# A down projection in passes of 256 tokens instead of 512

## The chip, the cores and the metric

The kernel runs on one NeuronCore of a Trainium2 chip. The metric is the time of one execution on the device, in microseconds (us). Three runs of the kernel before took 884.18, 884.53 and 885.38 us, so the median is 884.53 us. A fourth execution was recorded by the hardware profiler, and every line called a line of the profile comes from it.

Engine names are those of the profile: PE is the matrix engine and PEld its weight loads, DVE the vector engine, ACT the scalar engine, POOL the general one, and SP the engine that issues most DMAs. PSUM is the memory that PE writes its products to; it is cut into banks of 512 fp32 numbers per partition.

## The reference

One decoder layer in fp32, with 512 tokens and 1024 model columns. It has two feed-forward blocks (SwiGLU) with a mixing stage between them. Cut to what matters here:

```python
D_MODEL, SEQ = 1024, 512
D_FF = 256 * math.ceil(8 * D_MODEL / 3 / 256)            # 2816 = 22 tiles of 128

def swiglu(x, w_gate, w_up, w_down):
    return (jax.nn.silu(x @ w_gate) * (x @ w_up)) @ w_down

x = x + 0.5 * swiglu(rms_norm(x, g_ffn1), w_ffn1_gate, w_ffn1_up, w_ffn1_down)
h = rms_norm(x, g_mix); proj = h @ w_in
x = x + concat([attention(proj), conv(proj), memory_attention(proj, mem)]) @ w_out
x = x + 0.5 * swiglu(rms_norm(x, g_ffn2), w_ffn2_gate, w_ffn2_up, w_ffn2_down)
```

The change touches only `... @ w_down`, the down projection of both blocks.

## The kernel before, in words

**Layout.** Activations lie transposed, features in partitions and tokens along the row: `x` is 8 tiles of 128 features by 512 tokens. A product of a weight tile (128 by 128, loaded into PE) with an activation tile streams the tokens past the weights; one such instruction is called a pass here, and its width is the number of tokens.

**Three passes for fp32.** Each fp32 operand is split into a high part in the type `float32r` and the rest, `hi` and `lo` (`whi`/`wlo` for weights; `xh`/`xl`, `hh`/`hl`, `bh`/`bl` for activations). A product is then `whi*hi + whi*lo + wlo*hi`, three passes into the same PSUM bank. The function `mm3` (line 334) does this for a list of contraction tiles `k`; its passes are lines 337, 338 and 339. Before every pass PE loads that pass's weights, also where the pass before used the same ones.

**A feed-forward block** (`ffn`, line 389) walks over 22 hidden tiles `f`. The first 4 are plain: 8 contraction tiles by three passes of 512 tokens for gate and as many for up. The other 18 go through `fast` (line 443), which works on blocks of 256 tokens: seven products of 4 contraction tiles by 3 passes, all of width 256, made by `product` (line 434, passes on lines 439, 440 and 441). Their results go to PSUM banks that ACT copies out (lines 450, 454, 456, 468, tiles called `kept`) and DVE combines (lines 459, 470, 474). The hidden tile is split into `hh` and `hl` (lines 397, 398), 512 tokens each.

**The down projection** (`down`, line 479) is cut into six rounds of 4, 4, 4, 4, 2 and 4 hidden tiles. In each round every one of the 8 tiles `d` of `x` takes one bank from a ring of four (`mm_bank`), gets `mm3` over the round's hidden tiles, and DVE adds half of the bank to `x` (line 496). A step over 4 hidden tiles is thus 12 passes. The steps of a round are spread over the hidden tiles `f` of the next round, between the products of `fast`; the last round comes at the end of the block. In the very last step of the kernel (tile 7, last round, second block) the tokens are already cut in two: two banks, one for each half of the tokens, 12 passes of width 256 each.

**Weights** come by DMA in pieces of 128 by 1024 fp32, are split by ACT (line 165, `whi`) and DVE (line 166, `wlo`) a few pieces ahead of use, and lie in a ring of four pairs of buffers. The start of a buffer is shifted by 0 or 128 bytes (`off`); `fast` and `down` both use 128. In the built program the tiles `hh`, `hl`, `bh` and `bl` all start at byte 320 modulo 512 of their partition, also at token 256, and the weight tiles of both stages at byte 128 or 384 modulo 512.

**Order.** The code is written for a tile framework that puts each engine's instructions in order by its own estimate of when each can run, and sets the semaphores. PE, DVE and ACT each run their instructions strictly in that order.

Of the kernel before, what the change touches and what calls it, by code (L numbers as in the profile page):

```python
# [38 lines left out]
P = 128  # L39
T = 512  # L40
# [146 lines left out]
def per_load(r):  # L187

    return 8 // (ROUNDS[r][1] - ROUNDS[r][0])
# [14 lines left out]
def layer(tc, ctx, a):  # L204
    nc = tc.nc
    PE, ACT, DVE, POOL = nc.tensor, nc.scalar, nc.vector, nc.gpsimd
# [12 lines left out]
    def mm_bank():  # L219
        return psum.tile([P, T], F32, tag="mm", name=nm("mm"), bufs=4)  # L220
# [7 lines left out]
    def work():  # L228
        return tmp.tile([P, T], F32, tag="t", name=nm("t"), bufs=5)
# [101 lines left out]
            DVE.tensor_tensor(yy, yy, h, op=ALU.mult)  # L331
            DVE.scalar_tensor_tensor(out, yy, 1.5, out, op0=ALU.add, op1=ALU.mult)

    def mm3(ps, wh, wl, ks, hi, lo, first, last, woff=0):
        for i, k in enumerate(ks):
            w = slice((k - woff) * P, (k - woff + 1) * P)
            PE.matmul(ps, wh[:, w], hi(k), start=first and i == 0, stop=False)  # L337
            PE.matmul(ps, wh[:, w], lo(k), start=False, stop=False)  # L338
            PE.matmul(ps, wl[:, w], hi(k), start=False, stop=last and i == len(ks) - 1)  # L339

    xhk = lambda k: xh[k]
    xlk = lambda k: xl[k]
# [1 line left out]
    def scaled_split(d, gcol):  # L344

        g = par[:, gcol + d : gcol + d + 1]
        xh[d], xl[d] = atile("xh"), atile("xl")
        ACT.activation(xh[d], x[:, d], AF.Identity, scale=g)
        DVE.scalar_tensor_tensor(xl[d], x[:, d], g, xh[d].bitcast(F32), op0=ALU.mult, op1=ALU.subtract)  # L349
# [39 lines left out]
    def ffn(pool, norm, first, gain, hooks, next_gain, last):  # L389
# [89 lines left out]
        def down(r, g):  # L479

            lo, hi = ROUNDS[r]
            end = r == len(ROUNDS) - 1
            wh, wl = W.next()

            def step(j):
                d = g * per_load(r) + j
                cut = last and end and d == KT - 1
                for t0, t1 in [(0, T // 2), (T // 2, T)] if cut else [(0, T)]:
                    ps = mm_bank()[:, : t1 - t0]
                    mm3(  # L490
                        ps, wh, wl, range(lo, hi), lambda k: h_hi[k][:, t0:t1], lambda k: h_lo[k][:, t0:t1],
                        True, True, woff=lo - j * (hi - lo),
                    )
                    xd = x[:, d, t0:t1]
                    o = work()[:, : t1 - t0] if last and end else xd
                    DVE.scalar_tensor_tensor(o, ps, 0.5, xd, op0=ALU.mult, op1=ALU.add)  # L496
                    if last and end:
                        nc.sync.dma_start(a["out"][d, :, t0:t1], o)
                if end and not last:
                    nxt.add(d)  # L500
                    scaled_split(d, next_gain)

            return [lambda j=j: step(j) for j in range(per_load(r))]
# [4 lines left out]
        for f in range(NF):  # L508
# [4 lines left out]
            if f >= N_DIRECT:  # L513
                fast(f, mid)
            else:
                g, u = (sc_bank(), sc_bank()) if f % 3 == 2 else (mm_bank(), mm_bank())
                gh, gl = W.next()
                if f == 0:
                    uh, ul = W.next()
                    for ks in first:  # L520
                        mm3(g, gh, gl, ks, xhk, xlk, ks[0] == 0, ks[-1] == 7)
                        mm3(u, uh, ul, ks, xhk, xlk, ks[0] == 0, ks[-1] == 7)
                    norm.stats()
                    held = (g, u)
                else:
                    mm3(g, gh, gl, range(8), xhk, xlk, True, True)
                    if f == 1:
                        norm.spread()
                        raw[0] = evac(0, *held)
                        blocks(0)  # L530
                        hidden(0, raw[0])
                    uh, ul = W.next()
                    mm3(u, uh, ul, range(8), xhk, xlk, True, True)
                    raw[f] = evac(f, g, u)
                    if f == 1:
                        hidden(1, raw[1])
                    blocks(f)
                if f == N_DIRECT - 1:
                    for i in range(2, N_DIRECT):
                        hidden(i, raw[i])  # L540
# [666 lines left out]
```

## Time and profile before

| | us |
|---|---|
| median of three runs | 884.53 |
| the profiled execution | 884.99 |
| its span, first to last instruction | 883.2 |
| PE busy | 869.9 (98%) |
| PE weight loads busy | 760.4 (86%) |
| DVE busy | 713.1 (81%) |
| ACT busy | 438.2 (50%) |

Matmuls overlap in the profile: each is shown with its whole latency, so the busy times of groups on PE add up to more than the span. What a pass costs in a stream of passes is the distance from its start to the start of the next. Rows of the timeline give starts in us with two decimals; over a run of many passes, first start to last start divided by the number of passes is exact to a fraction of a nanosecond.

The two feed-forward blocks take most of the span: their passes over hidden tiles begin at 59.0 us in the first block and about 584 us in the second, and the mixing stage lies between about 370 and 517 us.

### The profile page before, as it was taken

Reading aid. Unit: us, or ns where it says so; the run is one execution under the profiler, and the core shown is the slowest. Engines: PE = TensorE matmul, PEld = TensorE weight load, DVE = VectorE, ACT = ScalarE, POOL = GpSimd, SP = SyncE. Lnnn points to the kernel's source line nnn. Section 1 sums busy time; section 2 is a strip of 40 time slices with the busy share of each in tenths; the row PEclk is TensorE's granted clock in tenths of the full one; section 3 lists DMA queues with packets and bytes.
Section 4 is the critical chain, followed back from the end, with each engine's and each line's share of the span. In section 5 each row is a group of like instructions: output and inputs, shape, how many; then the busy total and the mean of one; then the engine's idle time right before and its main releaser. Section 6 shows DMA issues by size and latency. Waiting matters only on the chain.

```text
span 883.2 us, 13993 instructions
## 1 busy us (share of the span) xinstructions
PE 869.9 (98%) x5522; PEld 760.4 (86%) x5525; DVE 713.1 (81%) x1121; ACT 438.2 (50%) x733; POOL 45.9 (5%) x38
## 2 busy tenths in 40 slices
PE   7999999999999999999999999999999999999998
PEld 3889999899999999888666788889999999989997
DVE  7999978986796886769999776999987878777872
ACT  6454554454563445533929754345554444534540
POOL 6000000000020000300020021000000000000000
PEclk9999999999999999999999999999999999999999
DMA  5522333333334244231010232323334332332312
GB/s 196 167 96 86 106 120 108 109 108 119 119 121 129 87 120 144 72 101 60 4 57 13 84 100 92 96 72 124 104 107 120 96 118 85 111 117 72 120 48 96
DMA packets 34082, 88.45 MB, mean 100 GB/s; under 512 B 3168, under 2 KB 7008, under 8 KB 34016
## 3 DMA queue, kind: packets, MB, share of 16 engines
q1 hardware_dynamic: 32864, 85.99, 30.9%
q10 hardware_dynamic: 1152, 1.57, 0.6%
q8 instruction: 43, 0.70, 0.3%
q14 instruction: 23, 0.19, 0.1%
HBM read 85.45 MB, written 2.10 MB: 99 GB/s over the span
## 4 chain that ended last, share of the span: by engine, by line
PE 93%; DVE 4%; DMA 1%; issue 1%; ACT 0%; SPq 0%; DVEq 0%
PE mm L337 15%; PE mm L339 15%; PE mm L338 15%; PE mm L439 11%; PE mm L441 11%; PE mm L440 11%; PE sc L439 2%; PE sc L441 2%; PE sc L440 2%; PE sc L337 1%; PE sc L339 1%; PE sc L338 1%; PE tp L924 1%; PE sc L863 1%; DVE conv L788 1%
## 5 line engine op out<-in xcount | busy, mean ns | idle before, releaser
L439 PE MATMUL mm<-bh,whi 128*128 128x256 f32 x864 | 239.8, 278 | 0.7 <-ACT kept L450 0.4
L441 PE MATMUL mm<-bh,wlo 128*128 128x256 f32 x864 | 239.2, 277 | 0.0
L440 PE MATMUL mm<-bl,whi 128*128 128x256 f32 x864 | 239.2, 277 | 0.0
L165 ACT CAST whi<-wraw 128x1024 fp32r<-128x1024 f32 (+2 forms) x122 | 124.3, 1021 | 125.2 <-PE mm L338 54.2
L166 DVE TENSOR_TENSOR wlo<-wraw,whi 128x1024 fp32r<-128x1024 f32 (+2 forms) x122 | 144.8, 1189 | 31.6 <-ACT whi L165 31.3
L439 PEld LDWEIGHTS mm<-bh,whi 128*128 128x128 f32 x864 | 162.3, 188 | 2.2 <-ACT kept L450 0.6
L440 PEld LDWEIGHTS mm<-bl,whi 128*128 128x128 f32 x864 | 162.7, 188 | 1.2
L441 PEld LDWEIGHTS mm<-bh,wlo 128*128 128x128 f32 x864 | 162.2, 188 | 0.0
L339 PE MATMUL mm<-hh,wlo 128*128 128x512 f32 (+1 forms) x356 | 139.4, 393 | 0.0
L338 PE MATMUL mm<-hl,whi 128*128 128x512 f32 (+1 forms) x356 | 139.4, 393 | 0.0
L337 PE MATMUL mm<-hh,whi 128*128 128x512 f32 (+1 forms) x356 | 138.6, 392 | 0.0
L166 DVE TENSOR_TENSOR wlo<-s,whi 128x1024 fp32r<-128x1024 f32 x72 | 88.4, 1229 | 28.7 <-ACT whi L165 28.5
L165 ACT CAST whi<-s 128x1024 fp32r<-128x1024 f32 x72 | 75.5, 1050 | 52.7 <-PE mm L440 36.5
L339 PEld LDWEIGHTS mm<-hh,wlo 128*128 128x128 f32 x356 | 66.9, 188 | 15.4
L339 PE MATMUL mm<-xh,wlo 128*128 128x512 f32 x192 | 76.4, 398 | 2.8 <-DVE wlo L178 2.8
L337 PEld LDWEIGHTS mm<-hh,whi 128*128 128x128 f32 x356 | 66.9, 188 | 13.5
L338 PEld LDWEIGHTS mm<-hl,whi 128*128 128x128 f32 x356 | 67.0, 188 | 13.4
L338 PE MATMUL mm<-xl,whi 128*128 128x512 f32 x192 | 75.9, 395 | 1.9 <-DVE xl L349 1.7
L337 PE MATMUL mm<-xh,whi 128*128 128x512 f32 x192 | 76.6, 401 | 0.6 <-ACT whi L177 0.6
L496 DVE SCALAR_TENSOR_TENSOR x<-mm,x 128x512 f32<-128x512 f32 x88 | 59.5, 684 | 9.9 <-PE mm L339 9.7
L460 ACT ACTIVATE t<-t 128x512 f32<-128x512 f32 x36 | 22.8, 632 | 56.2 <-DVE t L459 56.2
L165 ACT CAST vhi<-wraw 128x512 fp32r<-128x512 f32 x36 | 22.3, 621 | 52.6 <-PE sc L440 38.2
(245 smaller groups left out, 1395.7 us busy)
## 6 DMA issues: line engine op xcount, KB each, us to landing
wraw<-in_wgu SPq DMA_DIRECT2D x86, 512.0 KB, 3.5
wraw<-in_wd SPq DMA_DIRECT2D x44, 512.0 KB, 3.6
wraw<-in_win SPq DMA_DIRECT2D x12, 512.0 KB, 3.5
out<-t SPq DMA_DIRECT2D x7, 256.0 KB, 2.0
x<-in_xT SPq DMA_DIRECT2D x3, 512.0 KB, 5.9
wraw<-in_wout_a SPq DMA_DIRECT2D x6, 256.0 KB, 2.6
t<-in_memT ACTq DMA_DIRECT2D x4, 256.0 KB, 3.2
wraw<-in_wmk SPq DMA_DIRECT2D x2, 512.0 KB, 4.0
```

The source lines that it names most:

```text
L165: nc.scalar.copy(hi[:, :cols], raw[:, :cols])
L166: nc.vector.tensor_tensor(lo[:, :cols], raw[:, :cols], hi[:, :cols].bitcast(F32), op=ALU.subtract)
L337: PE.matmul(ps, wh[:, w], hi(k), start=first and i == 0, stop=False)
L338: PE.matmul(ps, wh[:, w], lo(k), start=False, stop=False)
L339: PE.matmul(ps, wl[:, w], hi(k), start=False, stop=last and i == len(ks) - 1)
L439: PE.matmul(ps, wh[:, c], bh[k][:, block], start=one, stop=False, skip_group_check=not first)
L440: PE.matmul(ps, wh[:, c], bl[k][:, block], start=False, stop=False, skip_group_check=not first)
L441: PE.matmul(ps, wl[:, c], bh[k][:, block], start=False, stop=end, skip_group_check=not first)
L460: ACT.activation(g, g, AF.Silu)
L496: DVE.scalar_tensor_tensor(o, ps, 0.5, xd, op0=ALU.mult, op1=ALU.add)
L788: DVE.scalar_tensor_tensor(conv[:, i], pad[:, i, j : j + T], w(i, j), conv[:, i], op0=ALU.mult, op1=ALU.add)
L863: PE.matmul(banks[h][:, i * ML + c.start : i * ML + c.stop], self.q[rows, n * P : (n + 1) * P], self.kt[rows, ks], start=not self.win, sto ...
```

## The change

`mm3` gets a parameter `cut`. With `cut=2` it runs its whole list of passes over the first half of the tokens, into the first half of the bank, and then the whole list again over the second half of the tokens, into the second half of the same bank. `down` asks for `cut=2` in every step of 512 tokens; the last step of the kernel, which is already cut, stays as it is, and so does every other caller. Only the first pass of the first half carries the start flag of the bank. DVE's addition still reads the whole bank, after both halves.

```diff
-    def mm3(ps, wh, wl, ks, hi, lo, first, last, woff=0):
-        for i, k in enumerate(ks):
-            w = slice((k - woff) * P, (k - woff + 1) * P)
-            PE.matmul(ps, wh[:, w], hi(k), start=first and i == 0, stop=False)
-            PE.matmul(ps, wh[:, w], lo(k), start=False, stop=False)
-            PE.matmul(ps, wl[:, w], hi(k), start=False, stop=last and i == len(ks) - 1)
+    def mm3(ps, wh, wl, ks, hi, lo, first, last, woff=0, cut=1):
+
+        n = ps.shape[-1] // cut
+        for c in range(cut):
+            t = slice(c * n, (c + 1) * n)
+            for i, k in enumerate(ks):
+                w = slice((k - woff) * P, (k - woff + 1) * P)
+                one, end = first and i == c == 0, last and i == len(ks) - 1
+                PE.matmul(ps[:, t], wh[:, w], hi(k)[:, t], start=one, stop=False, skip_group_check=cut > 1)
+                PE.matmul(ps[:, t], wh[:, w], lo(k)[:, t], start=False, stop=False, skip_group_check=cut > 1)
+                PE.matmul(ps[:, t], wl[:, w], hi(k)[:, t], start=False, stop=end, skip_group_check=cut > 1)
...
                         ps, wh, wl, range(lo, hi), lambda k: h_hi[k][:, t0:t1], lambda k: h_lo[k][:, t0:t1],
-                        True, True, woff=lo - j * (hi - lo),
+                        True, True, woff=lo - j * (hi - lo), cut=(t1 - t0) // (T // 2),
```

In the changed kernel the passes of `mm3` are lines 342, 343 and 344, and every later line number is higher by 5.

The order of PE's instructions, at one down step in the round over the second group of hidden tiles (one of the steps that stand between the products of `fast`), before:

```order
L337 MATMUL mm_1856<-hh_817,whi_1763 128x512 [waits PE_49]
L338 MATMUL mm_1856<-hl_818,whi_1763 128x512
L339 MATMUL mm_1856<-hh_817,wlo_1764 128x512 [waits DVE_49]
L337 MATMUL mm_1856<-hh_966,whi_1763 128x512
...
L339 MATMUL mm_1856<-hh_1238,wlo_1764 128x512
L439 MATMUL sc_1758<-bh_349,vhi_1794 128x256
```

and the same step now (numbers of tiles differ between the two programs):

```order
L342 MATMUL mm_2024<-hh_889,whi_1931 128x256 [waits PE_49]
L343 MATMUL mm_2024<-hl_890,whi_1931 128x256
L344 MATMUL mm_2024<-hh_889,wlo_1932 128x256 [waits DVE_49]
L342 MATMUL mm_2024<-hh_1050,whi_1931 128x256
...
L344 MATMUL mm_2024<-hh_1334,wlo_1932 128x256
L342 MATMUL mm_2024<-hh_889,whi_1931 128x256
L343 MATMUL mm_2024<-hl_890,whi_1931 128x256
...
L344 MATMUL mm_2024<-hh_1334,wlo_1932 128x256
L444 MATMUL sc_1926<-bh_349,vhi_1962 128x256
```

The 12 passes of 512 became 24 of 256, the whole list for one half and then the whole list for the other; the waits stand where they stood, none is added, and the product that follows is the same. PE has 6323 rows where it had 5279, which is 1044 more.

Because the framework's own estimates change, a few instructions of DVE and ACT change places. The largest such place that lies beside a wait of PE is on DVE in the first block, where the angles for the rotary embedding are made (lines 696 to 706 of the kernel before, tiles `t`) while a down step is added to `x`. Before:

```order
L470 TENSOR_TENSOR t_1599<-kept_1597,mm_1593 128x512
L701 SCALAR_TENSOR_TENSOR t_1570<-t_1573,t_1570 128x512
L166 TENSOR_TENSOR wlo_1708<-s_29_1682,whi_1707 128x1024
L702 SCALAR_TENSOR_TENSOR t_1570<-t_1571,t_1570 128x512
L474 TENSOR_TENSOR t_1599<-t_1599,t_1598 128x512
L703 TENSOR_SCALAR t_1570<-t_1570 128x512
L496 SCALAR_TENSOR_TENSOR x<-mm_1742,x 128x512
L398 TENSOR_TENSOR hl_1739<-t_1599,hh_1738 128x512
L166 TENSOR_TENSOR wlo_1764<-wraw_1604,whi_1763 128x1024
```

and now:

```order
L475 TENSOR_TENSOR t_1743<-kept_1741,mm_1737 128x512
L707 SCALAR_TENSOR_TENSOR t_1714<-t_1715,t_1714 128x512
L166 TENSOR_TENSOR wlo_1864<-s_29_1826,whi_1863 128x1024
L708 TENSOR_SCALAR t_1714<-t_1714 128x512
L479 TENSOR_TENSOR t_1743<-t_1743,t_1742 128x512
L501 SCALAR_TENSOR_TENSOR x<-mm_1898,x 128x512
L166 TENSOR_TENSOR wlo_1932<-wraw_1748,whi_1931 128x1024
L711 TENSOR_SCALAR t_1715<-t_1715 128x512
L403 TENSOR_TENSOR hl_1895<-t_1743,hh_1894 128x512
```

The last multiply-add of line 701 now stands ahead of the combination of the up half (line 470, now 475), line 702 (now 707) ahead of a weight split, and the rest of the hidden tile (`hl`) is made two places later. The second block's DVE order is unchanged.

## The prediction
> **What bounds the kernel now.** I read the page first: busy time, and by engine the chain of waits.
>
> ```profile
> span 883.2 us, 13993 instructions
> PE 869.9 (98%) x5522; PEld 760.4 (86%) x5525; DVE 713.1 (81%) x1121; ACT 438.2 (50%) x733; POOL 45.9 (5%) x38
> PE 93%; DVE 4%; DMA 1%; issue 1%; ACT 0%; SPq 0%; DVEq 0%
> ```
>
> PE sets the end: 93% of the chain is PE's own work. What a pass costs in the stream is then nearly all that counts. Next the groups on PE with shapes kept apart, for how many passes the change touches.
>
> ```profile
> L439 PE MATMUL mm<-bh,whi 128*128 128x256 f32 x864 | 239.8, 278 | 0.7 <-ACT kept L450 0.4 <-ACT kept L454 0.3
> L337 PE MATMUL mm<-hh,whi 128*128 128x512 f32 x348 | 136.4, 395 | 0.0
> L337 PE MATMUL mm<-hh,whi 128*128 128x256 f32 x8 | 2.2, 281 | 0.0
> ```
>
> Lines 338 and 339 have 348 each too: 1044 passes of 512 in the down projection, each to become two of 256. By the mean durations this looks like ruin (two times 278 or 281 ns for one of 395), but those are latencies that overlap. The cost is start to start, so I went to the timeline and took first and last starts of runs.
>
> First, a down step and the 60 products behind it:
>
> ```profile
> 209.73 0.39 PE L337 MATMUL mm<-hh,whi 128*128 128x512 f32 x1
> ...
> 212.53 0.28 PE L439 MATMUL mm<-bh,whi 128*128 128x256 f32 x1
> ...
> 219.33 0.39 PE L337 MATMUL mm<-hh,whi 128*128 128x512 f32 x1
> ```
>
> 12 passes of 512 in 2.80 us: 233.3 ns each. 60 passes of 256 in 6.80 us: 113.3 ns, less than half of 233.3. But the same products also run at another pace:
>
> ```profile
> 134.79 0.28 PE L439 MATMUL mm<-bh,whi 128*128 128x256 f32 x1
> ...
> 141.86 0.39 PE L337 MATMUL mm<-hh,whi 128*128 128x512 f32 x1
> ```
>
> 60 passes in 7.07 us: 117.8 ns, more than half. I call these the fast and the slow pace. The mean duration of a group tells which one rules, 276 ns or 281 ns. And the one place where the down projection already runs in halves is the end of the kernel, lines 337 to 339 with 256 tokens, behind 102 passes of 512:
>
> ```profile
> 853.27 0.39 PE L337 MATMUL mm<-hh,whi 128*128 128x512 f32 x1
> ...
> 877.07 0.28 PE L337 MATMUL mm<-hh,whi 128*128 128x256 f32 x1
> ...
> 879.77 0.28 PE L339 MATMUL mm<-hh,wlo 128*128 128x256 f32 x1
> ```
>
> 102 passes of 512 in 23.80 us: 233.3 ns again. 23 distances of 256 in 2.70 us: 117.4 ns, the slow pace. So **the question is which pace the halves will run at**: the exchange is 233.3 for 226.6 or for 235.
>
> **What decides the pace.** Where is each found, and what stands at the switch?
>
> ```profile
> L337 PE MATMUL mm<-hh,whi 128*128 128x512 f32 x24 | 9.5, 394 | 0.0
> L440 PE MATMUL mm<-bl,whi 128*128 128x256 f32 x72 | 20.2, 281 | 0.0
> L440 PE MATMUL sc<-bl,vhi 128*128 128x256 f32 x12 | 3.4, 281 | 0.0
> ...
> L337 PE MATMUL mm<-hh,whi 128*128 128x512 f32 x72 | 28.4, 395 | 0.0
> L440 PE MATMUL mm<-bl,whi 128*128 128x256 f32 x152 | 42.0, 276 | 0.0
> L440 PE MATMUL sc<-bl,vhi 128*128 128x256 f32 x28 | 7.7, 276 | 0.0
> ...
> L337 PE MATMUL mm<-hh,whi 128*128 128x512 f32 x136 | 53.2, 395 | 0.0
> L440 PE MATMUL mm<-bl,whi 128*128 128x256 f32 x388 | 107.1, 276 | 0.0
> L440 PE MATMUL sc<-bl,vhi 128*128 128x256 f32 x64 | 17.7, 276 | 0.0
> ...
> L337 PE MATMUL mm<-hh,whi 128*128 128x512 f32 x36 | 14.2, 395 | 0.0
> L440 PE MATMUL mm<-bl,whi 128*128 128x256 f32 x45 | 12.6, 281 | 0.0
> L440 PE MATMUL sc<-bl,vhi 128*128 128x256 f32 x8 | 2.2, 281 | 0.0
> ```
>
> These are the groups by window: 125 to 172.6 us (slow), 172.6 to 285 (fast), 583 to 833.4 (fast), 833.4 to the end (slow). One and the same code, with tiles at the same places, runs for 250 us at one pace and then at the other; so it is a state that PE keeps, not a property of the tiles. It changes where PE was held up:
>
> ```profile
> 833.35 0.28 PE L441 MATMUL mm<-bh,wlo 128*128 128x256 f32 x1
> 833.47 0.32 PE L439 MATMUL mm<-bh,whi 128*128 128x256 f32 x1
> 833.63 0.28 PE L440 MATMUL mm<-bl,whi 128*128 128x256 f32 x1
> ...
> 170.51 0.38 PE L439 MATMUL mm<-bh,whi 128*128 128x256 f32 x1 [0.36 <-ACT kept L450]
> 172.50 0.39 PE L439 MATMUL mm<-bh,whi 128*128 128x256 f32 x1 [0.30 <-ACT kept L454]
> ```
>
> At 833.47 a distance of 160 ns, some 47 too long, ends the fast pace; at 172.50 a wait for ACT of 0.30 us ends the slow one, while one of 0.36 us at 170.51 had left it as it was. And once a single pass of 512, alone between products, switches it:
>
> ```profile
> 242.77 0.28 PE L439 MATMUL mm<-bh,whi 128*128 128x256 f32 x1
> ...
> 246.85 0.39 PE L337 MATMUL mm<-hh,whi 128*128 128x512 f32 x1
> 247.08 0.28 PE L439 MATMUL mm<-bh,whi 128*128 128x256 f32 x1
> ...
> 249.91 0.39 PE L338 MATMUL mm<-hl,whi 128*128 128x512 f32 x1
> ```
>
> 36 products in 4.08 us (113.3), the one pass, then 24 products in 2.83 us (117.9). Elsewhere inside the two fast windows steps of an even number of passes stand between the products, and the pace behind them is what it was. My reading, an inference and not a measurement: halves of `hh` keep whatever pace they meet, as the products do, since their tiles have the same place modulo 512 bytes. The end of the kernel, slow since 833.63, agrees with it and doesn't prove it.
>
> **The change, term by term.** Passes that become pairs: 24 of line 337 in the first slow window and 36 in the last, times three lines, are 180 in slow surroundings; the other 864 are in fast ones.
>
> Fast: 864 x (233.3 - 2 x 113.3) = 864 x 6.7 ns = 5.8 us gained. Slow: 180 x (2 x 117.8 - 233.3) = 180 x 2.3 ns = 0.4 us lost. Sum: 5.4 us less. All of it lies on PE, which sets the end.
>
> Were no half to find the fast pace, 1044 x 2.3 = 2.4 us lost; were all to find it, 1044 x 6.7 = 7.0 us gained. These are the two bounds of the price.
>
> The Trainium skill speaks against the change: its page "TensorE: Matmul & The Clock Gate", section "Back-to-back issue gap", gives the warm distance as N/2.4 plus 2.5 ns. That is 215.8 ns for 512 and 109.2 for 256, so cutting would cost 2.5 ns per pair, by an estimate 2.6 us in all. Neither row agrees in size (233.3, 113.3 or 117.8), and the fast one contradicts the sign; the slow one fits the sign.
>
> The extra 1044 weight loads and passes ask nothing new of PE's supply: long runs of 256 already go at these paces. The bank is held as long as before, and the evacuation (line 496) still starts after the last pass. The changed places on DVE cost nothing where DVE has slack:
>
> ```profile
> 125.00:172.60 47.60, 46.94 (x326) 43.33 (x325) 40.86 (x60) 22.80 (x37) 0.00 (x0) 1.00 0.37 107
> 583.00:833.40 250.40, 250.40 (x1772) 231.75 (x1770) 202.38 (x267) 122.25 (x183) 0.00 (x0) 1.00 0.33 104
> ```
>
> In order: length, busy PE, PEld, DVE, ACT, POOL, then the clock, 1.00. PE is never idle for 250 us in the second block, and DVE has 48 us to spare. In the first window PE idles 0.66 us behind the angles of the rotary embedding; with one DVE operation more or less in front of it (about 0.6 us) that is the price, either way, of the reordering there. I take nothing.
>
> Against the profiled execution (884.99) the sum gives 879.6. The median of the runs is 0.46 lower, so I predict 879.3 us.
>
> **The rivals.** Each differs in which pace holds where.
>
> *Slow from the start of the second block.* Halves do not switch the pace, so whatever comes out of the plain stage at 584 us would last. If it is slow, the 136 x 3 = 408 fast passes there lose 9.0 ns instead (2.3 + 6.7), 3.7 us, and the (388 + 64) x 3 = 1356 products, fast today, lose 4.5 ns each, 6.1 us: 879.6 + 9.8 = 889.4, slower by 4.4 than the profiled execution. For it: today each run is preceded by passes of 512, which vanish as a reset. Against it: in today's window from 583 us the products come out fast from the start, behind an even number of passes. It decides at the first halves.
>
> *Slow after the rotary wait.* The wait at 172.50 might leave slow instead of fast until 285 us. The 72 x 3 = 216 passes there lose 1.9 us against the forecast and (152 + 28) x 3 = 540 products 2.4 us: 883.9, no change. For it: the wait at 170.51 changed nothing, so such a wait needn't help.
>
> *Halves of the down projection are always slow.* Then the end of the kernel is the rule for `hh`, at 117.4 to 117.8 ns, and the products keep theirs: 1044 x 1.5 to 2.3 ns is 1.6 to 2.4 us, so 887.0. The fixed cost per pass that the Trainium skill states would come out here too. Against it: at the end the products before it were slow already.
>
> *Fast everywhere.* If the two waits that start the slow windows fall away, 180 x 9.0 ns and 3 x (72 + 12 + 45 + 8) = 411 products x 4.5 ns come on top, 3.5 us: 876.1.
>
> That the change is not carried out is excluded: PE has 1044 more instructions in the order of the changed program.
>
> **How the numbers follow.** Forecast 0.46, fast everywhere 0.08, slow after the rotary wait 0.17, halves always slow 0.11, slow second block 0.18. The range, 876.0 to 889.5, holds all five central values; mixtures and the ends beyond are the rest. The forecast's own range is 878 to 881. About 0.2% (1.8 us) is what a measurement of this kernel can tell from no change. Faster by more: 0.54 (the first two). Within: 0.17. Slower: 0.29 (the last two).
>
> **What would show it.** Lines 342 to 344 with 256 tokens at a mean of 276 ns, and runs of 24 in 2.72 us instead of 2.80, show the main term right. A mean of 281 over most of the second block, products included, shows the slow second block. Halves at 281 between products at 276 show the third rival and that the pace belongs to the tiles. The prediction is wrong if the pace turns out to be set elsewhere than at waits and odd passes of 512, or if PE, now faster, begins to wait for banks, for ACT's copies or for weights: idle time in front of lines 444 or 342.

## The result, and the profile after

The changed kernel takes **892.22 us** (median of 22 runs); the kernel before, run beside it, takes 884.62 us (22 runs). The ratio is 1.0066, with a 95% interval of 1.0045 to 1.0087: slower by more than a measurement of this kernel needs to tell. Ratios in this document go by means, not medians, and leave out runs more than 1.5% above the fastest of their kernel (here two of the changed kernel, 897.38 and 903.36 us). The forecast was 879.3, the range ended at 889.5.

The runs of the changed kernel that are compared also lie further apart, from 883.1 to 895.0 us, where those of the kernel before lie from 883.1 to 886.7. The profiled execution took 894.95 us. Its page, busy time, the chain of waits by engine, and the groups that the change touches:

```profile
span 893.2 us, 16076 instructions
PE 877.8 (98%) x6566; PEld 814.4 (91%) x6569; DVE 713.4 (80%) x1121; ACT 438.8 (49%) x733; POOL 45.7 (5%) x38
PE 89%; DVE 6%; ACT 2%; issue 1%; DMA 1%; SPq 0%; ACTq 0%
L444 PE MATMUL mm<-bh,whi 128*128 128x256 f32 x864 | 241.5, 279 | 0.4 <-ACT kept L455 0.3
L343 PE MATMUL mm<-hl,whi 128*128 128x256 f32 x704 | 197.3, 281 | 4.0 <-DVE hl L403 4.0
L344 PE MATMUL mm<-hh,wlo 128*128 128x256 f32 x704 | 196.9, 280 | 0.0
```

PE still sets the end, but its share of the chain fell from 93% to 89% and DVE's rose. Line 343 now has 4.0 us of idle time in front of it, behind DVE's `hl`. That wait is in no row of the kernel before. The timeline of PE says where it stands, once in each block:

```profile
59.08 0.28 PE L342 MATMUL mm<-hh,whi 128*128 128x256 f32 x1
...
62.37 0.28 PE L445 MATMUL sc<-bl,vhi 128*128 128x256 f32 x1
64.89 0.58 PE L343 MATMUL mm<-hl,whi 128*128 128x256 f32 x1 [2.25 <-DVE hl L403]
65.27 0.42 PE L344 MATMUL mm<-hh,wlo 128*128 128x256 f32 x1
65.49 0.42 PE L342 MATMUL mm<-hh,whi 128*128 128x256 f32 x1
...
68.26 0.28 PE L344 MATMUL mm<-hh,wlo 128*128 128x256 f32 x1
...
588.78 0.28 PE L445 MATMUL sc<-bl,vhi 128*128 128x256 f32 x1
590.83 0.39 PE L343 MATMUL mm<-hl,whi 128*128 128x256 f32 x1 [1.77 <-DVE hl L403]
591.06 0.28 PE L344 MATMUL mm<-hh,wlo 128*128 128x256 f32 x1
```

Both places are in the **first down round**, over hidden tiles 0 to 3, of which tiles 2 and 3 have only just been made. Read it by starts. From 62.37 to 65.27 two passes take 2.90 us, where two fast ones take 0.23: 2.67 lost. From 588.78 to 591.06 the same: 2.05 lost. And from 65.27 to 68.26 there are 14 distances of 213.6 ns, nearly twice 113.3: 1.4 us lost. The last is the clock. The table of that stretch, with the columns as in the prediction (the seventh is the granted clock):

```profile
64.80:68.80 4.00, 3.91 (x20) 3.91 (x21) 3.25 (x5) 1.05 (x1) 0.00 (x0) 0.57 0.00 0
```

DVE did not get later. It makes `hl` of hidden tile 2 at the same time in both kernels; before, then after:

```profile
64.09 0.69 DVE L398 TENSOR_TENSOR hl<-kept,hh 128x512 fp32r<-128x512 f32 x1
```

```profile
64.16 0.68 DVE L403 TENSOR_TENSOR hl<-kept,hh 128x512 fp32r<-128x512 f32 x1
```

It is PE that comes earlier. Next the pace, by groups and window: 100 to 280 us, 323 to 369 us, and 606 to 826 us.

```profile
L342 PE MATMUL mm<-hh,whi 128*128 128x256 f32 x187 | 51.6, 276 | 0.0
...
L342 PE MATMUL mm<-hh,whi 128*128 128x256 f32 x76 | 21.4, 281 | 0.0
...
L342 PE MATMUL mm<-hh,whi 128*128 128x256 f32 x208 | 58.4, 281 | 0.0
L444 PE MATMUL mm<-bh,whi 128*128 128x256 f32 x356 | 100.0, 281 | 0.0
```

Fast in most of the first block, slow at its end, and slow in the second block from 591 us on, halves and products alike.

By stages, from the starts of passes (the first row of a block is six of the eight steps of round 0, 72 passes of 512 or 144 halves, after which products begin):

| stage | before, us | after, us | difference |
|---|---|---|---|
| block 1, round 0 | 59.0 to 75.8: 16.8 | 59.1 to 79.7: 20.6 | +3.8 |
| block 1, rest | 294.1 | 290.9 | -3.2 |
| mixing, plain stage of block 2 | 214.7 | 214.9 | +0.2 |
| block 2, round 0 | 584.6 to 601.4: 16.8 | 585.5 to 604.6: 19.1 | +2.3 |
| block 2, rest to the end of the span | 281.8 | 288.6 | +6.8 |

The two spans differ by 10.0 us, and the terms give nearly that. I counted the distances of 116 to 120 ns from one pass of 256 to the next pass, without those directly behind a pass of 512 (called slow distances from here on): 617 before, 2986 after. So: 1044 cut passes at the fast pace gain 7.0; 2369 more slow distances of 4.5 ns lose 10.7; the two hold-ups lose 4.7; the low clock 1.4. Sum +9.8.

### The profile page after: what moved, and what is told of

It reads as the page before. It is cut to its first block, busy times and chain, and to the rows that moved or that the text cites. A ratio compares the mean times of both kernels' runs of the same rounds, so it can differ in the third digit from the quotient of the medians.

```text
span 893.2 us, 16076 instructions
## 1 busy us (share of the span) xinstructions
PE 877.8 (98%) x6566; PEld 814.4 (91%) x6569; DVE 713.4 (80%) x1121; ACT 438.8 (49%) x733; POOL 45.7 (5%) x38
## 4 chain that ended last, share of the span: by engine, by line
PE 89%; DVE 6%; ACT 2%; issue 1%; DMA 1%; SPq 0%; ACTq 0%
PE mm L344 14%; PE mm L342 14%; PE mm L343 14%; PE mm L444 11%; PE mm L446 11%; PE mm L445 11%; PE sc L446 2%; PE sc L444 2%; PE sc L445 2%; PE tp L929 1%; PE sc L342 1%; PE sc L344 1%; PE sc L343 1%; PE sc L868 1%; DMA x<-in_xT 1%
## 5 line engine op out<-in xcount | busy, mean ns | idle before, releaser
L343 PE MATMUL mm<-hl,whi 128*128 128x256 f32 x704 | 197.3, 281 | 4.0 <-DVE hl L403 4.0
L344 PE MATMUL mm<-hh,wlo 128*128 128x256 f32 x704 | 196.9, 280 | 0.0
L342 PE MATMUL mm<-hh,whi 128*128 128x256 f32 x704 | 196.1, 280 | 0.0
L343 PEld LDWEIGHTS mm<-hl,whi 128*128 128x128 f32 x704 | 134.3, 191 | 4.5 <-DVE hl L403 4.4
L344 PEld LDWEIGHTS mm<-hh,wlo 128*128 128x128 f32 x704 | 133.4, 190 | 0.0
L342 PEld LDWEIGHTS mm<-hh,whi 128*128 128x128 f32 x704 | 132.4, 189 | 0.1
L344 PEld LDWEIGHTS mm<-xh,wlo 128*128 128x128 f32 x192 | 36.5, 190 | 11.8 <-DVE wlo L178 3.8
```

The lines of the kernel that those rows point to most:

```text
L342: PE.matmul(ps[:, t], wh[:, w], hi(k)[:, t], start=one, stop=False, skip_group_check=cut > 1)
L343: PE.matmul(ps[:, t], wh[:, w], lo(k)[:, t], start=False, stop=False, skip_group_check=cut > 1)
L344: PE.matmul(ps[:, t], wl[:, w], hi(k)[:, t], start=False, stop=end, skip_group_check=cut > 1)
```

## The experiments

Each median below stands with its ratio to the kernel before, which was run beside it on the same chip (884.68 to 885.02 us). In the first four expectations, theory A is the missed wait of round 0 with what follows it, theory B that halves are dear wherever they stand. Extra passes in the experiments go into banks that nobody reads; apart from them every kernel computes the whole layer.

### Where the loss sits: round 0 alone, all but round 0

**All but round 0 cut** (852 passes):

```diff
-  True, True, woff=lo - j * (hi - lo), cut=(t1 - t0) // (T // 2),
+  True, True, woff=lo - j * (hi - lo), cut=(t1 - t0) // (T // 2) if r else 1,
```

> The change without its first round: in round 0 of both blocks the passes stay 512 wide, in the five other rounds they are cut (852 of 1044). Theory A (the loss of the change is the wait of PE for hl in round 0, the lower clock behind it and the slow pace that the wait leaves; halves themselves are cheap): no wait over 0.3 us in round 0, the second block fast from its start, 672 pairs gain 6.7 ns and 180 lose 2.3: about 880.5 us (879 to 882), runs as close together as those of the kernel before. Theory B (halves of the down projection are dear wherever they stand): 852 x 2.3 ns more, 886.6 us or above.

Measured: 881.61 us, ratio 0.9976 (0.9959 to 0.9993). **Faster than before.** No wait for `hl` is left, and from 620 to 880 us halves and products run fast:

```profile
L444 PE MATMUL mm<-bh,whi 128*128 128x256 f32 x388 | 107.3, 277 | 1.4 <-DVE x L501 0.7 <-ACT kept L459 0.6
L342 PE MATMUL mm<-hh,whi 128*128 128x256 f32 x288 | 79.5, 276 | 0.0
```

The 1.4 us in front of line 444 are a wait for DVE's additions and one for ACT's copies: a faster PE begins to run into them. The runs lie between 878.7 and 887.7 us, further apart than those of the kernel before (883.4 to 887.9), against the expectation. So the spread does not end with the wait for `hl`; where it comes from here was not traced.

**Only round 0 cut** (192 passes): the same line with `cut=1 if r else (t1 - t0) // (T // 2)`.

> The other part of the change alone: only the 192 passes of round 0 are cut, all later rounds stay 512 wide. Theory A: first block's round 0 about 3.8 us longer and second block's about 2 us longer, as in the changed kernel; 890 us if the pace behind it is fast, up to 897 if the 1512 products of the second block become slow (4.5 ns each); runs spread by some us. Theory B: 192 x 2.3 ns, 885 us.

Measured: 889.08 us, 1.0063 (1.0035 to 1.0092). The wait is there in full, and the products of the second block stay fast (606 to 880 us); first the page's group, then the window's:

```profile
L343 PE MATMUL mm<-hl,whi 128*128 128x512 f32 (+1 forms) x420 | 150.7, 359 | 4.0 <-DVE hl L403 4.0
```

```profile
L444 PE MATMUL mm<-bh,whi 128*128 128x256 f32 x432 | 119.3, 276 | 0.0
```

So 18% of the cut passes carry the loss, and theory B falls: cutting the other 852 gains. In this execution, with 213 slow distances, hold-ups and low clock, not a slow pace, make the loss.

### The same, by block

Round 0 left whole in block 1 alone (`if r or last else 1`), and in block 2 alone (`cut=1 if last and r == 0 else ...`):

> The change, with the first down round left 512 wide in the first block alone. Theory A (the wait for `hl` and the slow passes behind it cost 3.8 us in block 1; block 2 has its own wait of 1.8 and, after it, a pace that nothing resets): 892.2 - 3.8 = 888.4, no wait at 65 us, a wait of about 1.8 us at 591. Rival (what block 1 loses is made up later, and the pace of block 2 is all): 892.

> The change, with the first down round left 512 wide in the second block alone. Theory A: the kernel with both rounds whole (881.6) and the loss of block 1 on top, 3.8 us: 885.4, with the second block fast throughout. Rival (the form of this round has nothing to do with the pace behind it, and only its wait of 1.8 us goes): 892.2 - 1.8 = 890.4.

Measured: whole in block 1, 884.6 us, 1.0013 (0.9987 to 1.0038); whole in block 2, 885.35 us, 1.0002 (0.9979 to 1.0026). The waits are where they were expected, one each; around 65 us with block 2 whole, around 586 us with block 1 whole:

```profile
PE mm L343 <- DVE hl L403: 2.3, 1, 2.3
```

```profile
PE mm L343 <- DVE hl L403: 1.8, 1, 1.8
```

The 885.35 is what theory A gave (885.4). The other, 884.6, is 3.8 under the 888.4 expected, which lies just outside its interval (883.6 to 888.1): I had assumed a slow second block behind that wait, and in the traced execution it is fast. Each round costs 3 to 4 us on top of the 881.6; together that gives 888.3, and the changed kernel's 892.2 is 3.9 above it, about as much as the intervals of the four kernels allow together.

### What makes PE wait: the cover in front of `hl`

**Both halves of each pass side by side** instead of one list after the other; all 1044 passes are cut:

```diff
-        for c in range(cut):
-            for i, k in enumerate(ks):
-                ... whi*hi, whi*lo, wlo*hi of half c
+        for i, k in enumerate(ks):
+            for x, y in ((wh, hi), (wh, lo), (wl, hi)):
+                for c in range(cut):
+                    ... x*y of half c
```

> All 1044 passes cut, but the two halves of one pass stand side by side (first half, second half, then the next pass) instead of the whole list for one half and then for the other. Theory A: in round 0 the passes that can run before hl is there are as long as before, 28 x 2 x 113 ns = 6.3 us, so no wait; halves in the fast pace: 5 us less, 879 to 880 us, little spread. Theory B, or if the order of the halves does not matter: 890 us or above with the wait still there.

Measured: 889.74 us, 1.0075 (1.0047 to 1.0102). The wait for `hl` is gone, and yet it is no faster. Here the second block is slow: round 0 begins fast and turns at 587.85 us, where the trace has one distance of 123 ns instead of 113 (a weight load that came 10 ns late for a pass with `hl`). Groups of 582 to 587.8 us, then of 588 to 880 us:

```profile
L342 PE MATMUL mm<-hh,whi 128*128 128x256 f32 x20 | 3.4, 276 | 0.0
...
L442 PE MATMUL mm<-bh,whi 128*128 128x256 f32 x432 | 121.4, 281 | 0.0
L342 PE MATMUL mm<-hh,whi 128*128 128x256 f32 x320 | 63.8, 281 | 0.0
```

So wait and pace are two losses. This kernel has the second without the first, the one with only round 0 cut the first without the second. I count 2970 slow distances here, about as many as in the changed kernel's first profile. The wait went as theory A said, but its 879 to 880 took the fast pace for granted and was missed by 10 us. All six runs lie between 888.4 and 896.3 us.

**`hl` made earlier**, everything cut as in the change:

```diff
+                    if f == N_DIRECT - 1:
+                        for i in range(2, N_DIRECT):
+                            hidden(i, raw[i])
                     blocks(f)
-                if f == N_DIRECT - 1:
-                    for i in range(2, N_DIRECT):
-                        hidden(i, raw[i])
```

> The change, with `hidden` of tiles 2 and 3 called ahead of `blocks(3)` instead of behind it: DVE makes `hl` of tile 2 eight operations earlier and that of tile 3 ahead of the block sums, and the passes of the first down round find them ready. Theory A (the waits come from the halved cover in front of `hl`): no wait of PE over 0.5 us at 65 and 591 us, so 892.2 less 4.1 us of waits and up to 1.7 us of slow passes behind them: 886.4 to 888.1, or less if the second block is then more often fast. Rival (DVE is late as a whole there): the wait goes over to the next thing that DVE makes, `bl` of tile 3, in front of the products at 76 us, and the time stays at 892.

Measured: **880.3 us, 0.9950 (0.9936 to 0.9965)**, the fastest kernel of all, and five runs within 2.0 us. The waits of PE around 65 and 588 us, then the page's group, then products between 600 and 825 us:

```profile
PE mm L343 <- DVE hl L403: 0.8, 1, 0.8
...
PE mm L343 <- DVE hl L403: 0.3, 1, 0.3
```

```profile
L343 PE MATMUL mm<-hl,whi 128*128 128x256 f32 x704 | 194.6, 277 | 1.2 <-DVE hl L403 1.2
```

```profile
L444 PE MATMUL mm<-bh,whi 128*128 128x256 f32 x384 | 106.0, 276 | 0.0
```

Two `hl` operations ahead of the block sums took back all that the change lost and left what it was to gain. The 0.8 us are above the 0.5 us expected: PE now reaches the `hl` of hidden tile 3 before DVE has made it. The rival (the wait goes over to the block sums) falls. The time is 6 us below my expectation, and in the traced execution no slow pace follows the waits; that a short hold-up leaves the pace alone is suggested by it, not shown.

### The pace: is it a draw?

The changed kernel itself, profiled twice more:

> The changed kernel itself, a second profiled execution. Theory A with the pace as a draw: round 0 of both blocks waits for `hl` again, 1.7 to 2.6 us each, while the pace behind the wait of block 2 need not be the slow one; the execution then ends near 892.4 - 9.9 = 882.5 if it is fast there, near 892 to 895 if it is slow. Rival (the change always leads to a slow second block): 892 to 895 and 281 ns in it.

> The changed kernel itself, a third profiled execution. The same two expectations as for the second.

Measured: 885.38 and 892.96 us. The waits are the same to 0.1 us in all three executions. The pace is not. Groups of 100 to 280 us and of 606 to 826 us, of the execution of 885.38 and then of that of 892.96:

```profile
L342 PE MATMUL mm<-hh,whi 128*128 128x256 f32 x186 | 51.3, 276 | 0.0
...
L342 PE MATMUL mm<-hh,whi 128*128 128x256 f32 x212 | 58.5, 276 | 0.0
```

```profile
L342 PE MATMUL mm<-hh,whi 128*128 128x256 f32 x176 | 49.5, 281 | 0.0
...
L342 PE MATMUL mm<-hh,whi 128*128 128x256 f32 x223 | 61.5, 276 | 0.0
```

| execution of the changed kernel | span, us | slow distances | where |
|---|---|---|---|
| first (894.95) | 893.2 | 2986 | 286 to 291, 324 to 370, 591 to the end |
| second (885.38) | 883.6 | 459 | 286 to 292, 834 to the end |
| third (892.96) | 891.2 | 2365 | 66 to 298, 841 to the end |

Slow pace begins behind the wait of block 2 in the first, behind the wait of block 1 in the third, behind neither in the second. The difference of 2527 slow distances between first and second is 11.4 us by 4.5 ns, and the spans differ by 9.6. So the rival "always a slow second block" falls, and the spread of the runs has a reason: with the same waits, the pace behind them differs from execution to execution of one program. By an estimate from these counts, an execution with both blocks slow would have a span of 893.2 + 1958 x 4.5 ns = 902.0 us (1958 are the third's slow distances from 66 to 298 us); the longest run of the changed kernel, 903.36 us, had one of 901.6, but was not traced.

The kernel before shows the same. Three of the kernels below differ from it in block 2 alone. From 125 to 174 us its profile, on which the prediction stands, has 242 slow distances, theirs have 13, 25 and 15. From 284 to 312 us all four have 176 or 177. So some slow stretches belong to the program, and the one from 125 us does not.

### What turns the pace

The prediction had inferred from one place that a single pass of 512 between products switches the pace. Four kernels test it, each with extra passes of 512 in block 2, behind the last step of round 0. The first adds one to the kernel before, with `hh` itself as the weights:

```diff
+            if last and f == N_DIRECT + 1:
+                PE.matmul(tp_bank(), h_hi[0][:, 0:P], h_hi[0], start=True, stop=True)
```

> The kernel before with one extra pass of 512 (a product into an unused bank, not part of the result) in the second block behind hidden tile 5. If an odd number of 512-wide passes turns the pace over, as read from the trace at 246.85 us, all products behind it until the next wait of PE (about 1200) run at 117.8 instead of 113.3 ns: 5.4 us more plus 0.2 for the pass, 890 us, and the mean of the products' group over that stretch is 281 ns. If the pace is set only by waits: 0.2 us more, 884.8.

Measured: 884.7 us, 0.9996 (0.9986 to 1.0007). Nothing turned; products between 628 and 825 us:

```profile
625.71 0.39 PE L545 MATMUL tp<-hh 128*128 128x512 f32 x1
```

```profile
L439 PE MATMUL mm<-bh,whi 128*128 128x256 f32 x326 | 90.0, 276 | 0.0
```

But its weights lay at byte 320 modulo 512, where no weight tile lies (that this is the reason was not shown). So, one pass with the step's own weights, and then two of them:

```diff
                     xd = x[:, d, t0:t1]
+                    if last and r == 0 and d == KT - 1:
+                        PE.matmul(tp_bank(), wh[:, :P], h_hi[0], start=True, stop=True)
```

> The kernel before with one pass of 512 more, in the second block: behind the last step of the first down round it repeats one of that step's weight tiles over `hh` of hidden tile 0, into a bank that nobody reads. Unlike the odd pass run earlier, its weights lie where all down weights lie. Theory P (an odd number of such passes turns the pace): the 1166 products that run fast between about 626 and 833 us turn slow, 4.5 ns each, 5.2 us, so 889 to 890. Rival (the pace is turned only where PE is held up, by however little): 0.2 us for the pass, so 884.9, and the products behind it at 276 ns as in the kernel before.

> The kernel before with two extra passes of 512 where the odd pass with its own weights had one, into two banks that nobody reads. Theory P (an odd number turns the pace, an even one turns it twice): 884.75 + 2 x 0.233 = 885.2, products at 276 ns from 627 us on as in the kernel before. Rival (an extra pass there disturbs the products, whatever the number): 890.3 or more, products at 281 ns.

Measured: one pass 890.27 us, 1.0059 (1.0044 to 1.0074); two passes 884.93 us, 1.0000 (0.9990 to 1.0010). **One pass of 0.23 us costs 5.5 us, two cost nothing that can be measured.** Products behind it (628 to 833, and 628 to 825 us), one pass, then two:

```profile
627.53 0.39 PE L495 MATMUL tp<-hh,whi 128*128 128x512 f32 x1
627.76 0.28 PE L439 MATMUL mm<-bh,whi 128*128 128x256 f32 x1
```

```profile
L439 PE MATMUL mm<-bh,whi 128*128 128x256 f32 x332 | 93.3, 281 | 0.0
```

```profile
L439 PE MATMUL mm<-bh,whi 128*128 128x256 f32 x330 | 91.1, 276 | 0.0
```

Both came out near what theory P said (889 to 890, and 885.2). And the same single pass in the changed kernel, where no other pass of 512 follows:

> The change, with the same extra pass of 512 as in the odd pass with its own weights, behind the last step of the first down round in block 2. Theory P (it turns the pace): where the second block has gone slow behind its wait it now turns fast from about 630 us on, 2207 passes times 4.5 ns, so 892.4 - 9.9 = 882.5; executions that were fast there turn slow, so the spread stays. Rival (only a hold-up turns the pace): 892.4, and passes of 281 ns before and behind the extra pass.

Measured: 894.22 us, 1.0123 (1.0089 to 1.0157). The second block was fast in this execution up to the pass at 627 us, and slow for all 2207 passes behind it (600 to 627, then 627.3 to 880 us):

```profile
L444 PE MATMUL mm<-bh,whi 128*128 128x256 f32 x48 | 13.2, 276 | 0.0
...
L444 PE MATMUL mm<-bh,whi 128*128 128x256 f32 x384 | 107.9, 281 | 0.0
```

The pass turned the pace, as theory P has it. The 882.5 I gave was wrong, because I took the second block for slow behind its wait. Two of the six runs, 901.28 and 901.79 us, are 8.8 and 9.3 us longer than the traced one; a slow first block, 1958 x 4.5 ns = 8.8 us by the estimate above, would be enough for that, but they were not traced.

A turn from slow to fast by an extra pass was not seen, but the prediction's own place at 246.85 us has one. The step there is split into 1 and 11 passes, and behind the 11, also an odd number, the products of the kernel before are fast again:

```profile
252.47 0.28 PE L439 MATMUL sc<-bh,vhi 128*128 128x256 f32 x1
...
255.19 0.39 PE L337 MATMUL mm<-hh,whi 128*128 128x512 f32 x1
```

24 passes in 2.72 us are 113.3 ns each, beside 117.9 ahead of the 11. The same double turn stands at this place in all five traces whose round there is uncut: the kernel before, the three with extra passes, and the one with only round 0 cut, with PE never idle between.

Even numbers kept the pace almost always, but not always. In the traces of the kernel before and of the experiments, 210 steps or parts of steps with an even number of passes of 512 stood between fast passes of 256, and the pace stayed; of 37 that began in the slow pace, 5 ended in the fast one, with PE never idle in the step.

## Why the prediction was wrong

**Right: PE sets the end, and the halves run at the pace of the products around them.** 276 ns beside 276 or 277, 281 beside 281, wherever the lines above show both. The fast term (6.7 ns per cut pass) stands: with `hl` in time the cut kernel takes 880.3, beside a forecast of 879.3.

**The step that failed: "The extra 1044 weight loads and passes ask nothing new of PE's supply", and "The changed places on DVE cost nothing where DVE has slack".** Both put at nothing a wait of PE for DVE. They were argued from slack over whole windows: the one from 125 us leaves round 0 of block 1 out, and in the one from 583 us the 48 us that DVE has to spare over 250 us say nothing about the first 7. At the start of round 0 DVE is less than 1 us ahead. The number was there to be worked out from the kernel before. Round 0 starts at 59.0 us, and `hl` of hidden tile 2 is finished at 64.09 + 0.69 = 64.78. Until then PE has, in each of its four banks, the six passes of tiles 0 and 1 and one pass with `hh` of tile 2: 28 passes. At 512 tokens they last 28 x 233.3 ns = 6.5 us, to 65.5, and cover DVE by 0.8 us. As halves, with the whole list of the first half ahead of the second and a bank's second half queued behind its first, 28 passes last 3.2 us; with two passes of a product (`sc`) that the framework put in between, PE is dry at 62.5 and waits 2.3 us. The same in block 2, 1.8 us. Measured with the slow first passes behind the waits: 4.7 us, and 1.4 us of low clock, 6.1 in all, more than the whole gain of 5.4 that was forecast. Passes of a product among the first halves, in the order of the changed program, were a sign of it that I did not price.

**Failed too: which passes are slow.** I took the windows of the kernel before (180 cut passes slow, 864 fast) as if they belonged to places in the program. In part they are a draw that can fall anew where PE is held up, and the change added two hold-ups. In the first profile this loses more, 10.7 us, than waits and clock together. The rival "slow from the start of the second block" (889.4, chance 0.18) is what the first profile shows, but only as one draw of several; its argument that the vanished passes of 512 matter is open.

**Right by inference: an odd pass of 512 turns the pace.** Shown with the step's own weights, twice, and by the split step near 247 us in five traces; with `hh` as the weights it did not, a condition that the prediction did not have. That an even number leaves the pace alone held for all steps that began fast, not for all that began slow.

**Right: nothing for the rotary embedding.** The products wait 0.4 us for ACT's copies, 0.7 before. But that wait differs between executions by more than this: at 171 to 174 us it is 1.7 and 1.8 us in two of the kernels whose first block is unchanged.

**The other rivals.** Halves that are always slow: refuted by 276 ns between products at 276. Slow behind the rotary wait: not seen in the first profile, fast there from 100 to 280 us. Fast everywhere: not seen, though the kernel with round 0 whole came near it, with 68 slow distances, and the one with round 0 whole in block 2, with 67. The formula of the Trainium skill that spoke against the change ("TensorE: Matmul & The Clock Gate", section "Back-to-back issue gap") would have made cutting dearer by 2.6 us, by the prediction's estimate; the page gives it for a single isolated matmul, which the prediction left out. The two kernels without the long waits gained 3.1 and 4.7 us (881.61 and 880.3 beside 884.68 and 885.02).

**Open.** What in a hold-up decides the pace. Of twelve traced waits of 1.8 to 2.3 us in round 0, two were followed by a slow block; one hold-up of 10 ns was too. Whether shorter waits draw less often was not tried by itself. Slow stretches also began at about 322 us and between 830 and 841 us in some executions of cut kernels, far from round 0, and why is not known either.

## What to carry to other kernels

When items in an in-order queue are cut in two and each half runs its whole list before the other, the work that stands in front of the first unready operand halves in time. Count it, pass by pass, at every place where the operands have only just been made, and compare it with the moment that the producer is done; a producer's slack over a whole stage says nothing about its start. And a gain of a few nanoseconds per instruction has to be checked against states that the instructions keep: look at more than one execution before calling them properties of the code.

## What the runs showed of the hardware that I had not expected

A stream of passes of 256 with a weight load each keeps one of two paces, 113.3 or 117.8 ns, for hundreds of microseconds. An odd number of passes of 512 between them turns it: all 12 cases with weights from a weight tile did, 7 from fast to slow and 5 back. An even number left a fast stream fast in 210 cases of 210, and a slow one slow in 32 of 37. It also turned behind some hold-ups of PE, once at a delay of 10 ns. One added pass of 0.23 us cost 5.5 us that way.

Six of the twelve waits of 1.8 to 2.3 us in round 0 were followed by a lower clock: 14 to 17 passes of 256 at about 213 ns (granted clock 0.57 over 4 us in the first profile). It came behind the wait of block 1 or that of block 2, never behind both. A wait of 0.8 us lowered nothing, and nor did one of 2.2 us at 171.7 us in the kernel with round 0 whole. The Trainium skill, "TensorE: Matmul & The Clock Gate", section "What's actually happening", has the clock fall after an idle window of about 3.4 us, and the same page, section "Back-to-back issue gap", gives N/1.2 for the lowered clock, 213.3 ns for 256. The trace agrees with the second; as to the first, idle times of 1.8 to 2.3 us were enough here in half of the cases.
